# A macaron transformer block: first gate/up sums read unsplit copies of x, and loads of operands and of w_out move on the queue

## The chip, the cores and the metric

One core of one Trainium2 chip runs the whole program in one launch. The metric is device time in microseconds (us); lower is better. Before: median 2323.25 us of three runs (2322.42 to 2323.91).

## The reference, cut to what matters

x is 1024 tokens by 1024 columns, float32.

```python
x = LN1(alpha*x + 0.5*FFN1(x))              # FFN: (silu(x @ w_gate) * (x @ w_up)) @ w_down, 4096 wide
z = x @ w_in                                # q, k, v of 8 heads of 64, and the inputs of an RG-LRU
fox = causal softmax attention of q, k, v with forget gates (a bias cum[t] - cum[s] on the scores)
lru = gelu(gate) * RG_LRU(conv(u))
x = LN2(alpha*x + concat(fox, lru) @ w_out)
x = LN3(alpha*x + 0.5*FFN2(x))
```

## The kernel before, in words

Every float32 operand of a matmul is split in two: hi, a rounded copy that ACT (the scalar engine) casts, and lo = source - hi, which DVE (the vector engine) subtracts. A product is then three matmuls of 128x512 on PE (the tensor engine), written in lines 163, 164 and 165: hi by hi and the two cross terms. The two big products gate and up of each FFN go by a Strassen-like scheme with seven products of half-size blocks in place of eight. For a pair of 128-column blocks of w_gate and w_up, `weights` loads 128x8x256 raw weights on SP's queue (L364; a load of w_gate and one of w_up), forms t1, t2, t3, t4 from the quarters (L355) and splits each (ACT L349, DVE L350). There are 16 such pairs; in pairs 1 to 15 only weights are new.

Pair 0, `first_pair`, also builds the block sums of x. The rows of x are loaded (x2 tiles and `row` tiles), transposed on PE through PSUM (L249, tile `b`), and split into "11", "12", "22", "21" and the sums s1 = 22 + 21 (L449), s2 = s1 - 11 (L475), s3 = 11 - 21 (L479), s4 = 12 - s2 (L519). The tiles A, As and As4 hold the splits; `put` casts hi at once and queues the lo subtraction, and `do` issues the next one queued (L391). For s2, s3 and s4, blocks "11" and "12" are transposed a second time (`a11`, `a12`), since their first transposes have left PSUM by then and only their splits remain. After the sums come the additions of the products into the results (L436, L523, L524, L533, L544), and behind them the finish of the pair's result: DVE multiplies gate by up (L692), forms block sums of it for the next product (L695 to L699), and POOL stores them. `first_pair` runs in the order in which it is written; other parts are ordered by the scheduler.

While gate/up 1 runs, idle slots of the other engines prepare operands of FFN 2 and of w_out in DRAM. A step of `prepare` loads two `aux` tiles on SP (L272), subtracts (L290, DVE), splits (L278 on ACT, L279 on DVE) and stores to pre_d or wo_d on POOL's queue (GpSimd). `ready_pair` at the start of FFN 2 loads pre_d back (L556), and `ready_out_w` (L1119) loads the eight split tiles `w` of wo_d, 512 KB each.

The attention runs its 8 heads of 8 query tiles as 64 units in one loop over n. A unit's scores are L1158 (with kh) and L1159 (with kl); POOL masks the bias tile `cum` (L1162), DVE takes p = scores + cum and its maximum m (L1164), ACT the exponential (L1165), PE transposes p (L1179), and L1200 multiplies by v. Each head's load is eight DMAs on SP's queue: q, kh, kl of two halves, cum, v. In between the loop fills in output-projection tiles of the LRU half (`fill`), loads `w` at n = 45, 47, 49, 51 and the stored `mix` tiles at n in MIXES, and runs `out_tile`, the output projection. POOL stores mix to mix_d (L1216) after subtracting (L1213).

SP and POOL issue their DMAs in the order of the program; a DMA that waits on SP holds those behind it.

Of the kernel before, what the change touches and what calls it, by code (L numbers as in the profile page):

```python
# [59 lines left out]
class Block:  # L60
# [273 lines left out]
    def gate_up(self, wg, wu, h_d, rows, bank, tp, wsp, raws=None, later=None, aside=None, ready=None, steps=None):  # L334
# [26 lines left out]
        def weights(pair, view, w):  # L361

            r = self.raw([P, KT, 2 * P])
            nc.sync.dma_start(r, view[:, :, pair * 2 * P:(pair + 1) * 2 * P])  # L364
            b11, b12, b21, b22 = quarters(r)
            w["11"] = parts(b11)
            w["21"] = parts(b21)
            t1 = less(b12, b11)
            t2 = less(b22, t1)
            w["t2"] = parts(t2)  # L370
            w["t1"] = parts(t1)
            w["t3"] = parts(less(b22, b12))
            w["22"] = parts(b22)
            w["t4"] = parts(less(b21, t2))

        def first_pair(g, u):

            both = g, u
            q = {m: quarters(r) for m, r in zip(both, raws)}
            r1, r2 = rows[0:4], rows[4:NT]  # L380
            late = []

            def put(to, src):
                hi, lo = to
                nc.scalar.copy(hi, src)
                late.append((lo, src, hi))

            def do(n=1):
                for _ in range(n):
                    lo, src, hi = late.pop(0)  # L390
                    v.tensor_tensor(lo, src, f32(hi), ALU.subtract)  # L391

            def place(name, j):
                return tuple(x[:, :, j * P:(j + 1) * P] for x in A[name])

            def fill(m, n, src):
                m.w[n] = homes[n, m] if (n, m) in homes else two_blocks()
                put(m.w[n], src)

            homes = {(n, m): two_blocks() for n in ("11", "21", "t1") for m in both}  # L400
            t21 = [block() for _ in range(4)]
            t1, t2, t4, t3 = {}, {}, {}, {}
            for j in range(4):
                put(place("11", j), self.transposed(r1[j], 0, bank))
                do()
            put(place("12", 0), self.transposed(r1[0], 1, bank))
            fill(g, "11", q[g][0])
            do()
            for j in (1, 2):
                put(place("12", j), self.transposed(r1[j], 1, bank))  # L410
                do()
            fill(u, "11", q[u][0])
            do()
            put(place("12", 3), self.transposed(r1[3], 1, bank))
# [9 lines left out]
            s = [block() for _ in range(4)]  # L424
            fill(g, "t1", t1[g])
            do()
            nc.scalar.copy(g.s1, g.sum)
            fill(u, "t1", t1[u])
            do()
            t2[g] = less(q[g][3], t1[g])  # L430
            do()
            t2[u] = less(q[u][3], t1[u])
            a22, two = {}, {}

            def add_two(m):
                v.tensor_tensor(m.c[0], two[m], m.s1, ALU.add)  # L436

            def put_22(*js):
                for j in js:
                    put(place("22", j), a22[j])  # L440

            for j in range(4):
                nc.scalar.copy(t21[j], self.transposed(r2[j], 0, bank))
                a22[j] = self.transposed(r2[j], 1, bank)
                if j == 0:
                    nc.scalar.copy(u.s1, u.sum)
                else:
                    put(place("s1", j - 1), s[j - 1])
                v.tensor_tensor(s[j], a22[j], t21[j], ALU.add)  # L449
                if j:  # L450
                    do()
            put(place("s1", 3), s[3])
            two[g] = g.product("21", "12")
            put_22(0)
            do(2)
            two[u] = u.product("21", "12")
            add_two(g)
            later()
            put_22(1, 2, 3)
# [12 lines left out]
            four = {g: g.product("t4", "22")}  # L472

            def s2(j):
                v.tensor_tensor(s[j], s[j], a11[j], ALU.subtract)  # L475
                put(place("s2", j), s[j])

            def s3(j):
                v.tensor_tensor(t21[j], a11[j], t21[j], ALU.subtract)  # L479
# [33 lines left out]
            fill(g, "22", q[g][3])  # L513
            do()
            fill(u, "22", q[u][3])
            do(2)
# [10 lines left out]
            s4(0)  # L527
            nc.scalar.copy(u.u, u.sum)
            g.product("t3", "s3", g.sum)
            s4(1)  # L530
            do()
            for m in both:
                v.tensor_tensor(m.u, m.u, m.s5, ALU.add)  # L533
            s4(2)
            do()
            u.product("t3", "s3", u.sum)
            s4(3)
            do()
            add_seven(g)
            do()  # L540
            three = {m: m.product("22", "s4") for m in both}
            add_seven(u)
            for m in both:
                v.tensor_tensor(m.c[1], three[m], m.u, ALU.add)  # L544

        def ready_pair(g, u):

# [15 lines left out]
            for n in ("t4", "t2"):  # L563
                r = self.rawp.tile([P, 4, 4, P], F32R, tag="raw", name=self.nm("raw"))
                for i, m in enumerate(both):
                    fetch(n, m, (r[:, 2 * i], r[:, 2 * i + 1]))
# [111 lines left out]
        def halves(r):  # L678
            return r[:, 0:H], r[:, H:]

        pending = None
        for pair in range(FF // P // 2):
            if pair == 0:
                g0, h0, first, fifth, g1, h1, u = (self.row() for _ in range(7))
                homes = list(zip(halves(first), halves(first), halves(fifth)))
                gate, up = Matrix((g0, g1), *homes[0]), Matrix((h0, h1), *homes[1])
# [35 lines left out]
            for m in (gate, up):  # L722
# [399 lines left out]
    def attention(self, w_out, mixp, ln, normed):  # L1122
# [7 lines left out]
        with self.pool("att_p", 3) as pp, self.pool("att_t", 1) as tp, self.pool("att_pt", 6) as ptp, self.pool("att_qk", 2, side="right") as qkp:  # L1130
# [110 lines left out]
            for n in range(len(units) + AHEAD + 1):  # L1241
# [173 lines left out]
```

## Time and profile before

| | us |
|---|---|
| median of the runs | 2323.25 |
| the profiled execution | 2323.19 |
| its span, first to last instruction | 2321.5 |
| PE busy | 2298.7 (99% of the span) |
| DVE busy | 1635.6 (70%) |
| ACT busy | 1019.1 (44%) |
| POOL busy | 227.8 (10%) |
| mean granted PE clock | 0.997 |

The profiled execution is 1.7 us longer than its span and 0.06 us under the median. In the timeline rows the columns are the start in us, the duration, the engine, the line, the operation and its tiles, a count of like instructions, and in brackets how long the engine stood idle before and what released it. A matmul's row lasts 0.39 us, but the next one starts 0.227 us after it; likewise a DVE row of 0.68 us is followed 0.60 us later. The lines are those of the kernel before; from about line 1000 on the changed kernel's are 10 higher.

### The profile page before, as it was taken

Reading aid. Unit: us, or ns where it says so; the run is one execution under the profiler, and the core shown is the slowest. Engines: PE = TensorE matmul, PEld = TensorE weight load, DVE = VectorE, ACT = ScalarE, POOL = GpSimd, SP = SyncE. Lnnn points to the kernel's source line nnn. Section 1 sums busy time; section 2 is a strip of 40 time slices with the busy share of each in tenths; the row PEclk is TensorE's granted clock in tenths of the full one; section 3 lists DMA queues with packets and bytes.
Section 4 is the critical chain, followed back from the end, with each engine's and each line's share of the span. In section 5 each row is a group of like instructions: output and inputs, shape, how many; then the busy total and the mean of one; then the engine's idle time right before and its main releaser. Section 6 shows DMA issues by size and latency. Waiting matters only on the chain.

```text
span 2321.5 us, 28560 instructions
## 1 busy us (share of the span) xinstructions
PE 2298.7 (99%) x10705; PEld 1914.1 (82%) x10705; DVE 1635.6 (70%) x2521; ACT 1019.1 (44%) x1623; POOL 227.8 (10%) x388
## 2 busy tenths in 40 slices
PE   8999999999999999999999999999999999999998
PEld 7888888888888888888898788888888888888887
DVE  7867666666467788866667899565656665577886
ACT  5443434343344345453556755334333333344341
POOL 0121111100000000111133210000000000000000
PEclk9999999999999999999999999999999999999999
DMA  4444444433276433233274934232323232564542
GB/s 150 141 141 145 139 147 141 146 113 125 101 259 234 147 127 109 75 92 110 91 218 126 283 137 141 86 118 89 122 93 123 87 118 87 195 244 168 182 144 73
DMA packets 194444, 323.08 MB, mean 139 GB/s; under 512 B 10033, under 2 KB 115825, under 8 KB 194305
## 3 DMA queue, kind: packets, MB, share of 16 engines
q1 hardware_dynamic: 167712, 230.74, 30.9%
q0 software_dynamic: 26592, 90.51, 9.9%
q8 instruction: 84, 1.38, 0.3%
q14 instruction: 56, 0.45, 0.1%
HBM read 226.81 MB, written 94.40 MB: 138 GB/s over the span
## 4 chain that ended last, share of the span: by engine, by line
PE 81%; issue 10%; DVE 3%; DMA 3%; POOL 2%; ACT 1%; SPq 0%; POOLq 0%; DVEq 0%; ACTq 0%
PE x L163 7%; PE x L164 7%; PE x L165 7%; PE s L165 6%; PE s L164 6%; PE s L163 6%; PE a L165 6%; PE a L164 6%; PE a L163 6%; PE b L163 6%; PE b L164 6%; PE b L165 6%; PE a L1200 1%; PE a L1179 1%; PE a L1049 1%
## 5 line engine op out<-in xcount | busy, mean ns | idle before, releaser
L349 ACT CAST ws<-t 128x512 fp32r<-128x512 f32 x240 | 148.9, 623 | 374.2 <-PE b L164 253.0
L349 ACT CAST ws<-raw 128x512 fp32r<-128x512 f32 x180 | 111.0, 622 | 239.3 <-PE x L164 237.3
L350 DVE TENSOR_TENSOR ws<-t,ws 128x512 fp32r<-128x512 f32 x240 | 164.3, 686 | 56.4 <-ACT ws L349 50.6
L350 DVE TENSOR_TENSOR ws<-raw,ws 128x512 fp32r<-128x512 f32 x180 | 123.3, 688 | 114.4 <-ACT ws L349 110.3
L164 PE MATMUL a<-ws,ws 128*128 128x512 f32 x512 | 199.8, 390 | 0.2
L163 PE MATMUL a<-ws,ws 128*128 128x512 f32 x512 | 199.3, 390 | 0.4 <-ACT row L672 0.4
L163 PE MATMUL b<-As,ws 128*128 128x512 f32 x512 | 199.4, 389 | 0.2 <-ACT row L663 0.2
L164 PE MATMUL b<-As,ws 128*128 128x512 f32 x512 | 199.3, 389 | 0.0
L165 PE MATMUL b<-As,ws 128*128 128x512 f32 x512 | 199.2, 389 | 0.0
L165 PE MATMUL a<-ws,ws 128*128 128x512 f32 x512 | 199.2, 389 | 0.0
L163 PE MATMUL x<-As,ws 128*128 128x512 f32 x504 | 196.6, 390 | 2.1 <-ACT row L659 2.0
L164 PE MATMUL x<-As,ws 128*128 128x512 f32 x504 | 196.1, 389 | 0.0
L165 PE MATMUL x<-As,ws 128*128 128x512 f32 x504 | 196.1, 389 | 0.0
L163 PE MATMUL x<-A,ws 128*128 128x512 f32 x496 | 193.3, 390 | 0.0
L165 PE MATMUL x<-A,ws 128*128 128x512 f32 x496 | 193.0, 389 | 0.0
L164 PE MATMUL x<-A,ws 128*128 128x512 f32 x496 | 193.0, 389 | 0.0
L772 ACT CAST ws<-raw 128x1024 fp32r<-128x1024 f32 x112 | 117.4, 1050 | 157.8 <-PE a L164 87.2
L775 DVE TENSOR_TENSOR ws<-raw,ws 128x1024 fp32r<-128x1024 f32 x112 | 136.6, 1220 | 53.0 <-ACT ws L772 52.6
L702 POOL DMA_DIRECT2D h_d<-row x96 | 68.9, 719 | 968.5 <-DVE row L696 928.4
L163 PE MATMUL s<-ws,ws 128*128 128x512 f32 x384 | 149.5, 389 | 0.0
L165 PE MATMUL s<-ws,ws 128*128 128x512 f32 x384 | 149.4, 389 | 0.0
L164 PE MATMUL s<-ws,ws 128*128 128x512 f32 x384 | 149.4, 389 | 0.0
(295 smaller groups left out, 5252.7 us busy)
## 6 DMA issues: line engine op xcount, KB each, us to landing
raw<-h_d SPq DMA_DIRECT2D x56, 1024.0 KB, 5.4
h_d<-row POOLq DMA_DIRECT2D x96, 512.0 KB, 3.5
wd<-in_ffn_w_down_dram SPq DMA_DIRECT2D x32, 1024.0 KB, 7.5
raw<-in_ffn_w_gate_dram SPq DMA_DIRECT2D x30, 1024.0 KB, 5.3
raw<-in_ffn_w_up_dram SPq DMA_DIRECT2D x30, 1024.0 KB, 5.3
h_d<-row POOLq DMA_DIRECT2D x32, 256.0 KB, 2.7
raw<-in_w_in_dram SPq DMA_DIRECT2D x16, 512.0 KB, 4.9
pre_d<-ws POOLq DMA_DIRECT2D x28, 256.0 KB, 2.7
```

Source lines behind the costliest of these rows:

```text
L163: mm(out, ah, bh, start=first, stop=False, skip_group_check=goes_on)
L164: mm(out, ah, bl, start=False, stop=False, skip_group_check=goes_on)
L165: mm(out, al, bh, start=False, stop=last, skip_group_check=goes_on)
L349: nc.scalar.copy(hi, src)
L350: v.tensor_tensor(lo, src, f32(hi), ALU.subtract)
L702: nc.gpsimd.dma_start(d[:, 2 * n:2 * n + 2], t.rearrange("p (r t) -> p r t", r=2))
L772: cast = nc.scalar.copy(hi, src)
L775: self.mark = v.tensor_tensor(lo, src, f32(hi), ALU.subtract)
L1049: nc.tensor.matmul(pa[:, 0:width], xh, wh[:, 0:width], start=k == 0, stop=False)
L1179: nc.tensor.transpose(pa[:, (j % 4) * P:(j % 4 + 1) * P], p[:, j * P:(j + 1) * P], self.ident)
L1200: mm(pv[:, ps], vt[:, j, :], pts[h, qt][j // 4][l][:, j % 4, ps], start=j == 0 and l == 0, stop=j == last and l == 1)
```

## The change

In `first_pair`, ACT keeps a plain copy of each first transpose of "11" and "12" in the row of x that it came from, and s2, s3 and s4 read these copies instead of second transposes. The product "22"·s4 adds onto the product "t1"·"s1" in PSUM (m.z), so that the two additions of L533 go; `add_two` and `add_seven` come behind s4. Steps of `prepare` are tied behind the latest raw weight load, `ready_pair`'s first loads behind a later one of the program, and the w_out tiles are loaded at n = 36 to 39.

```diff
             for j in range(4):
-                put(place("11", j), self.transposed(r1[j], 0, bank))
+                pt = self.transposed(r1[j], 0, bank)
+                put(place("11", j), pt)
+                nc.scalar.copy(unsplit(r1[j], 0), pt)
                 do()
...
+            def put_12(j):
+                keep.append((unsplit(r1[j], 1), self.transposed(r1[j], 1, bank)))
+                put(place("12", j), keep[-1][1])
+
+            def keep_12():
+                nc.scalar.copy(*keep.pop(0))
...
-            add_two(g)
...
-            a11 = [self.transposed(r1[j], 0, bank) for j in range(2)]
             u.z = u.product("t1", "s1")
-            add_two(u)
-            a11 += [self.transposed(r1[j], 0, bank) for j in (2, 3)]
...
-                v.tensor_tensor(s[j], s[j], a11[j], ALU.subtract)
+                v.tensor_tensor(s[j], s[j], unsplit(r1[j], 0), ALU.subtract)
...
-            a12 = [self.transposed(r1[j], 1, bank) for j in range(4)]
...
-                v.tensor_tensor(s[j], a12[j], s[j], ALU.subtract)
+                v.tensor_tensor(s[j], unsplit(r1[j], 1), s[j], ALU.subtract)
...
-            for m in both:
-                v.tensor_tensor(m.u, m.u, m.s5, ALU.add)
...
+            for m in both:
+                add_two(m)
             add_seven(g)
-            do()
-            three = {m: m.product("22", "s4") for m in both}
+            for m in both:
+                m.product("22", "s4", m.z)
             add_seven(u)
             for m in both:
-                v.tensor_tensor(m.c[1], three[m], m.u, ALU.add)
+                v.tensor_tensor(m.c[1], m.z, m.u, ALU.add)
...
-            for n in ("11", "21", "t1"):
-                for m in both:
-                    fetch(n, m, two_blocks())
+            with self.tc.issue_after(self.fetched.ins):
+                for n in ("11", "21", "t1"):
+                    for m in both:
+                        fetch(n, m, two_blocks())
...
                     if steps and step in ("two", "five"):
-                        next(steps, None)
+                        with self.tc.issue_after(self.weight_load.ins):
+                            next(steps, None)
...
-                if 45 <= n < 53 and n % 2:
+                if 36 <= n < 40:
                     w_fox.append(next(w_steps))
```

`fill(g, "22", ...)` and `fill(u, "22", ...)` also move two places down among the s4 steps.

On DVE, at the start of pair 0, where the last weights of "t1" are split (L391) and the sums s1 begin; before:

```order
L391 TENSOR_TENSOR ws_178<-raw_136,ws_177 128x512
L290 TENSOR_TENSOR aux_775<-aux_775,aux_773 128x256
L391 TENSOR_TENSOR ws_180<-t_261,ws_179 128x512
L355 TENSOR_TENSOR t_289<-raw_135,t_261 128x512
L391 TENSOR_TENSOR ws_182<-t_264,ws_181 128x512
L355 TENSOR_TENSOR t_292<-raw_136,t_264 128x512
L449 TENSOR_TENSOR ws_280<-b_300,ws_183 128x512
```

and now:

```order
L391 TENSOR_TENSOR ws_178<-raw_136,ws_177 128x512
L391 TENSOR_TENSOR ws_180<-t_265,ws_179 128x512
L355 TENSOR_TENSOR t_296<-raw_135,t_265 128x512
L391 TENSOR_TENSOR ws_182<-t_268,ws_181 128x512
L355 TENSOR_TENSOR t_299<-raw_136,t_268 128x512
L464 TENSOR_TENSOR ws_284<-b_307,ws_183 128x512
```

The step of `prepare` (L290) has left this place; it now stands in pair 1.

On DVE, where pair 0's result is finished and pair 1's operand t2 is split (the L350 row that reads the newest t); before, with L350 of t2 ahead of the last five additions L695 to L699:

```order
L692 TENSOR_TENSOR row_167<-row_167,row_166 128x1024
L350 TENSOR_TENSOR ws_684<-t_681,ws_683 128x512
L695 TENSOR_TENSOR row_168<-row_163,row_167 128x512
L696 TENSOR_TENSOR row_168<-row_163,row_167 128x512
L697 TENSOR_TENSOR row_162<-row_163,row_167 128x512
L698 TENSOR_TENSOR row_163<-row_163 128x512
L699 TENSOR_TENSOR row_167<-row_167 128x512
```

and now, where the same five are L704 to L708:

```order
L704 TENSOR_TENSOR row_168<-row_163,row_167 128x512
L705 TENSOR_TENSOR row_168<-row_163,row_167 128x512
L706 TENSOR_TENSOR row_162<-row_163,row_167 128x512
L707 TENSOR_TENSOR row_163<-row_163 128x512
L708 TENSOR_TENSOR row_167<-row_167 128x512
L355 TENSOR_TENSOR t_643<-raw_633 128x512
L666 TENSOR_TENSOR row_627<-b_723,row_628 128x512
L355 TENSOR_TENSOR t_645<-raw_633,t_643 128x512
L355 TENSOR_TENSOR t_655<-raw_633 128x512
L355 TENSOR_TENSOR t_665<-raw_633,t_645 128x512
L350 TENSOR_TENSOR ws_648<-t_645,ws_647 128x512
```

The five additions have moved ahead of t2 and its split.

On SP, behind the load of head 5 (heads are counted from 0), where the tiles of mix, w and head 6 (q, kh, kl, cum) are loaded; before:

```order
L1269 DMA mix_11083<-mix_d 128x1024
L1269 DMA mix_11084<-mix_d 128x1024
L1119 DMA w_11254<-wo_d 128x1024
L1119 DMA w_11255<-wo_d 128x1024
L1140 DMA kh_11106<-k_d 64x1024
L1139 DMA q_11105<-q_d 64x1024
L1141 DMA kl_11107<-k_d 64x1024
```

and now:

```order
L1129 DMA w_10944<-wo_d 128x1024
L1129 DMA w_10945<-wo_d 128x1024
L1129 DMA w_10969<-wo_d 128x1024
L1129 DMA w_10970<-wo_d 128x1024
L1129 DMA w_11007<-wo_d 128x1024
L1129 DMA w_11008<-wo_d 128x1024
L1129 DMA w_11027<-wo_d 128x1024
L1129 DMA w_11028<-wo_d 128x1024
L1279 DMA mix_11063<-mix_d 128x1024
L1279 DMA mix_11064<-mix_d 128x1024
L1149 DMA q_11085<-q_d 64x1024
L1150 DMA kh_11086<-k_d 64x1024
```

Six more loads of `w` stand ahead of head 6; the later places of `w`, behind heads 6 and 7, are empty.

More of the change, by code (lines that the diff above doesn't have):

```diff
@@ L363, in weights @@
             r = self.raw([P, KT, 2 * P])
-            nc.sync.dma_start(r, view[:, :, pair * 2 * P:(pair + 1) * 2 * P])
+            self.weight_load = nc.sync.dma_start(r, view[:, :, pair * 2 * P:(pair + 1) * 2 * P])
             b11, b12, b21, b22 = quarters(r)
@@ L403, in first_pair @@
             for j in range(4):
-                put(place("11", j), self.transposed(r1[j], 0, bank))
-                do()
-            put(place("12", 0), self.transposed(r1[0], 1, bank))
+                pt = self.transposed(r1[j], 0, bank)
+                put(place("11", j), pt)
+                nc.scalar.copy(unsplit(r1[j], 0), pt)
+                do()
+            keep = []
+            def put_12(j):
[3 more added lines that the diff above has]
+                nc.scalar.copy(*keep.pop(0))
+            put_12(0)
             fill(g, "11", q[g][0])
@@ L409, in first_pair @@
             for j in (1, 2):
-                put(place("12", j), self.transposed(r1[j], 1, bank))
+                put_12(j)
                 do()
@@ L413, in first_pair @@
             do()
-            put(place("12", 3), self.transposed(r1[3], 1, bank))
+            put_12(3)
             do(2)
@@ L424, in first_pair @@
             s = [block() for _ in range(4)]
+            keep_12()
             fill(g, "t1", t1[g])
@@ L428, in first_pair @@
             fill(u, "t1", t1[u])
+            keep_12()
+            keep_12()
             do()
@@ L446, in first_pair @@
                     nc.scalar.copy(u.s1, u.sum)
+                    keep_12()
                 else:
@@ L474, in s2 @@
             def s2(j):
-                v.tensor_tensor(s[j], s[j], a11[j], ALU.subtract)
+                v.tensor_tensor(s[j], s[j], unsplit(r1[j], 0), ALU.subtract)
                 put(place("s2", j), s[j])
             def s3(j):
-                v.tensor_tensor(t21[j], a11[j], t21[j], ALU.subtract)
+                v.tensor_tensor(t21[j], unsplit(r1[j], 0), t21[j], ALU.subtract)
                 put(place("s3", j), t21[j])
@@ L512, in first_pair @@
             do()
-            fill(g, "22", q[g][3])
             do()
-            fill(u, "22", q[u][3])
-            do(2)
             def s4(j):
-                v.tensor_tensor(s[j], a12[j], s[j], ALU.subtract)
+                v.tensor_tensor(s[j], unsplit(r1[j], 1), s[j], ALU.subtract)
                 put(place("s4", j), s[j])
@@ L527, in first_pair @@
             s4(0)
+            fill(g, "22", q[g][3])
             nc.scalar.copy(u.u, u.sum)
@@ L530, in first_pair @@
             s4(1)
-            do()
-            for m in both:
-                v.tensor_tensor(m.u, m.u, m.s5, ALU.add)
+            fill(u, "22", q[u][3])
+            do(2)
             s4(2)
@@ L537, in first_pair @@
             s4(3)
-            do()
+            do(3)
+            for m in both:
+                add_two(m)
             add_seven(g)
-            do()
-            three = {m: m.product("22", "s4") for m in both}
+            for m in both:
+                m.product("22", "s4", m.z)
             add_seven(u)
             for m in both:
-                v.tensor_tensor(m.c[1], three[m], m.u, ALU.add)
+                v.tensor_tensor(m.c[1], m.z, m.u, ALU.add)
         def ready_pair(g, u):
@@ L558, in fetch @@
                 m.w[n] = to
-            for n in ("11", "21", "t1"):
-                for m in both:
-                    fetch(n, m, two_blocks())
[L563 to L566, printed above, removed]
+            with self.tc.issue_after(self.fetched.ins):
+                for n in ("11", "21", "t1"):
+                    for m in both:
+                        fetch(n, m, two_blocks())
+                for n in ("t4", "t2"):
+                    r = self.rawp.tile([P, 4, 4, P], F32R, tag="raw", name=self.nm("raw"))
+                    for i, m in enumerate(both):
+                        fetch(n, m, (r[:, 2 * i], r[:, 2 * i + 1]))
             t21 = [block() for _ in range(4)]
@@ L684, in gate_up @@
                 g0, h0, first, fifth, g1, h1, u = (self.row() for _ in range(7))
-                homes = list(zip(halves(first), halves(first), halves(fifth)))
-                gate, up = Matrix((g0, g1), *homes[0]), Matrix((h0, h1), *homes[1])
+                gate, up = (Matrix((r, e), r[:, 0:H], x, y) for r, e, x, y in zip((g0, h0), (g1, h1), halves(first), halves(fifth)))
             else:
```

## The prediction

> **What bounds the kernel now.** I read the page first, then the waits of PE, then a table of windows, and last the timelines of the places that the diff touches.
>
> ```profile
> span 2321.5 us, 28560 instructions
> PE 2298.7 (99%) x10705; PEld 1914.1 (82%) x10705; DVE 1635.6 (70%) x2521; ACT 1019.1 (44%) x1623; POOL 227.8 (10%) x388
> ...
> PE b L163 <- ACT ws L443: 2.8, 1, 2.8
> PE s L1158 <- DVE m L1164: 2.4, 7, 0.9
> ...
> PE a L1179 <- DVE pt L1184: 1.0, 3, 0.6
> PE a L1179 <- ACT p L1165: 0.5, 1, 0.5
> ```
>
> PE is busy 2298.7 of 2321.5 us, so 22.8 us is all that better feeding could give. Its longest wait, 2.8 us, stands once, in gate/up 1's pair 0; the next ones are in the attention. These are the two places that the change touches on PE's path. The windows (us, PE, PEld, DVE, ACT, POOL busy, granted PE clock, DMA share, GB/s):
>
> ```profile
> 22.19:25.60 3.41, 1.41 (x6) 1.20 (x7) 3.32 (x7) 2.56 (x5) 0.00 (x0) 1.00 0.00 0
> 25.60:29.01 3.41, 3.41 (x10) 2.68 (x9) 2.97 (x5) 2.63 (x6) 0.00 (x0) 0.50 0.00 0
> 29.01:50.00 20.99, 20.99 (x104) 17.55 (x104) 19.59 (x33) 11.91 (x21) 0.00 (x0) 1.00 0.01 2
> 50.00:75.00 25.00, 24.73 (x114) 19.86 (x113) 24.78 (x40) 12.53 (x20) 2.94 (x4) 1.00 0.47 163
> 75.00:1290.00 1215.00, 1210.62 (x5712) 1012.37 (x5711) 844.86 (x1345) 544.17 (x875) 159.73 (x264) 1.00 0.43 140
> 1290.00:1345.00 55.00, 51.46 (x346) 43.82 (x345) 44.78 (x110) 40.39 (x99) 13.88 (x36) 1.00 0.91 285
> ```
>
> Two things to see. From 29 to 75 us DVE is nearly as full as PE (19.59 of 20.99, then 24.78 of 25.00), while over the next 1215 us it is at 70%: at the start two engines bound together. And after the window in which PE worked 1.41 of 3.41 us its clock was granted at 0.50 for one window of 3.41 us.
>
> **Gate/up 1, PE's side.** The chain ahead of the 2.80 us wait and the second transposes, in PE's, DVE's and ACT's timelines:
>
> ```profile
> 15.62 1.29 DVE L391 TENSOR_TENSOR ws<-raw,ws 128x512 fp32r<-128x512 f32 x2
> 19.57 0.43 DVE L290 TENSOR_TENSOR aux<-aux,aux 128x256 f32<-128x256 f32 x1 [2.66 <-DMA aux<-in_ffn_w_gate_dram]
> 19.91 0.68 DVE L391 TENSOR_TENSOR ws<-t,ws 128x512 fp32r<-128x512 f32 x1
> ...
> 23.56 0.58 ACT L443 COPY ws<-b 128x512 f32<-128x512 f32 x1
> ...
> 24.19 0.50 PE L163 MATMUL b<-A,ws 128*128 128x512 f32 x1 [2.80 <-ACT ws L443]
> ...
> 34.09 1.03 PE L249 MATMUL b<-ident,row 128*128 128x128 f32 x8
> ...
> 37.70 1.03 PE L249 MATMUL b<-ident,row 128*128 128x128 f32 x8
> ...
> 49.47 1.91 PE L249 MATMUL b<-ident,row 128*128 128x128 f32 x16
> ```
>
> DVE stood 2.66 us for the aux tiles of an operand step, whose loads SP had issued ahead; the sums s1, ACT's copies and PE's next product stood behind that. With the step tied behind the raw loads, L290 leaves this place: the 2.80 us go, and with them the idle window and the half clock, 3.41 x 0.5 = 1.7 us. The 32 second transposes go: 8, 8 and 16 of 0.109 us (34.09 to the next matmul is 0.87), 3.5 us. PE alone could be 2.8 + 1.7 + 3.5 = 8.0 us earlier. ACT's eight copies of 0.58 us (the L443 row has the shape) are 4.6 us; ACT is idle 9 us from 29.01 to 50.00 alone, so I cost them at nothing; without that cover they would hold the casts behind them, 4.6 us at most.
>
> **Gate/up 1, DVE's side.** DVE cannot follow by 8.0. The place where that shows is pair 1's operand t2, whose lo part the first L164 of its product reads:
>
> ```profile
> 28.51 0.69 DVE L436 TENSOR_TENSOR row<-b,row 128x512 f32<-128x512 f32 x1 [0.35 <-PE b L165]
> 31.56 0.69 DVE L436 TENSOR_TENSOR row<-b,row 128x512 f32<-128x512 f32 x1 [0.56 <-PE b L165]
> 38.34 0.69 DVE L475 TENSOR_TENSOR ws<-ws,b 128x512 f32<-128x512 f32 x1 [0.42 <-PE b L249]
> ...
> 52.17 1.29 DVE L533 TENSOR_TENSOR row<-row,row 128x512 f32<-128x512 f32 x2
> ...
> 64.47 1.22 DVE L692 TENSOR_TENSOR row<-row,row 128x1024 f32<-128x1024 f32 x1
> 65.61 0.68 DVE L350 TENSOR_TENSOR ws<-t,ws 128x512 fp32r<-128x512 f32 x1
> 66.21 0.68 DVE L695 TENSOR_TENSOR row<-row,row 128x512 f32<-128x512 f32 x1
> ...
> 68.27 0.39 PE L164 MATMUL x<-As,ws 128*128 128x512 f32 x1
> ```
>
> From the L391 at 19.91 up to t2's split at 65.61 the order of before has 67 rows of 0.60 us (65.61 to 66.21) and two of 1.14 (64.47 to 65.61): 42.5 of 45.7 us, 3.2 idle. The order of the changed kernel has 72 and two ahead of the same split: the two L533 (52.17) are gone, and the five finishing additions, an L666 and an L355 have moved ahead. That is 45.5 us. They can begin when the L391 of 15.62 ends, at 16.9 instead of 19.91. Of the idle time, 1.33 us (the three waits quoted) belongs to steps that are moved or read no transposes now; 1.9 stays. So the split stands at 16.9 + 45.5 + 1.9 = 64.3, done at 65.0, and PE's L164 comes at about 65.0 where it came at 68.27: a gain of 3.3 us, not 8.0. Bounds: with no idle at all 5.2, with all 3.2 of it again 2.0. I take 3.3, since the waits that remain are those of the same steps. From there DVE has 30% to spare again, and PE keeps what it has gained: nothing in pairs 1 to 15 gives it back, if the operand steps behind the raw loads wait no longer on DVE than that spare; without that cover each such wait costs up to the 2.66 us of L290.
>
> PE now has 8.0 - 3.3 = 4.7 us of waiting spread ahead of that split: by the same rows some in pair 1's first products, most ahead of t2's. If two us of it fall into one window, the row after 22.19:25.60 says that a half-clock window follows, 1.7 us. The windows do not start with the kernel's steps, so I take three chances in ten, 0.5 us. The Trainium skill (TensorE: Matmul & The Clock Gate, Part 1: The HAM clock gate) has the clock fall only after about one whole idle window of 3.4 us; by that rule this term is 0 and the sum 0.5 us lower. This trace speaks against it: 1.41 us of work in the window did not keep the clock.
>
> **Attention.** Head 6's cum from issue to landing, the two loads of w behind head 6 on SP and their time to landing, and the rate at a full DMA in two windows:
>
> ```profile
> 1298.93 9.90 DMA cum<-cum_d
> ...
> 1301.94 2.12 SPq L1119 DMA_DIRECT2D w<-wo_d  x2
> ...
> DMA to landing us min/median/max: 9.5/10.3/11.0
> ...
> 1301.00:1311.00 10.00, 9.20 (x63) 7.56 (x62) 8.87 (x26) 9.04 (x24) 3.08 (x9) 1.00 1.04 286
> 1310.30:1311.40 1.10, 1.10 (x9) 0.97 (x8) 0.99 (x6) 1.10 (x5) 0.73 (x2) 1.00 1.03 417
> ```
>
> Six more w tiles, 6 x 0.524 MB = 3.15 MB, stand ahead of head 6's load on SP, and DMA is full from there on (share over 1), so they cannot be hidden. At 417 GB/s, a stretch of such large rows, they take 7.5 us; at 286, a mixed stretch, 11.0. Head 6's cum landed at 1298.93 + 9.90 = 1308.8, and will land at 1316.3 to 1319.8. What it meets:
>
> ```profile
> 1313.11 1.23 DVE L1164 CUSTOM_DVE_ANT_0 p<-s,cum 128x1024 f32<-128x1024 f32 x1
> ...
> 1322.40 0.40 PE L1159 MATMUL s<-kl,q 128*128 128x512 f32 x1
> ...
> 1323.52 1.11 POOL L1216 DMA_DIRECT2D mix_d<-mix  x2
> 1324.64 0.30 POOL L1162 TENSOR_SCALAR_AFFINE_SELECT cum<-cum 128x128 f32<-128x128 f32 x1
> 1325.82 1.21 DVE L1164 CUSTOM_DVE_ANT_0 p<-s,cum 128x1024 f32<-128x1024 f32 x1
> ...
> 1338.20 0.50 PE L165 MATMUL a<-w,mix 128*128 128x512 f32 x1 [0.18 <-DMA mix<-mix_d]
> ```
>
> Head 6's first p ran at 1313.11 and will run at about 1316.3 + 0.3 for the mask: 3.5 us late. The order puts 2.2 us more of head 5's products ahead of head 6's scores, so PE has something to do meanwhile. Between this p and head 7's first, 12.7 us later, the order has only some 8 us of PE's work, so a delay of 3.5 can be made up there, and head 7 decides. Only four more w stand ahead of it (the order of before has two between the heads), 2.1 MB, 5.0 us at 417 GB/s; and of those two the second, landing 9.5 and 11.0 us after issues at 1301.9 and 1302.8, took 2.4 us where 0.524 MB take 1.3 at that rate. Without that loss the four cost 3.9. Head 7's first scores were through at 1322.40 + 0.40 = 1322.8, and yet p came at 1325.82, since POOL's mask at 1324.64 stood behind two stores of mix. In the new order those stores belong to values that come earlier, and POOL is free. So p comes at 1322.8 + 3.9 + 0.3 = 1327.0, 1.2 us late, or 2.3 with the loss. Behind it the way to the output projection is as long as before, and the wait for mix at 1338.20 (0.18 idle, some 0.3 against the cadence) goes, since no w stands ahead of that load. I take 0.9 of loss, at the rate that such large rows had. The bounds are -1 (PE's waits of 1.0 and 0.5 us for pt and p shrink by more than the loads cost) and +5 (286 GB/s).
>
> `ready_pair`'s eight loads, 2.1 MB, come behind all this, at 1335 to 1345:
>
> ```profile
> 1403.81 0.50 PE L163 MATMUL b<-A,ws 128*128 128x512 f32 x1
> ```
>
> Their first reader is FFN 2's first product at 1403.81; at 285 GB/s they need 7 us. Nothing.
>
> **The sum,** against the profiled execution's 2323.2 us (span 2321.5 and 1.7 around it; the median of the runs is the same to 0.1): -3.3 + 0.5 + 0.9 = -1.9, so 2321.3 us. About 0.2%, 4.65 us, is what a measurement of this kernel can tell from no change; the lines are at 2318.6 and 2327.9.
>
> **The rivals.** (1) DVE is no bound: it fills its idle time and the steps in front of t2 are not needed in that order, so that PE takes all 8.0. For it: 1.33 of DVE's waits are for PE itself. Against it: the count of 74 rows. Then 2323.2 - 8.0 + 0.9 = 2316.1. (2) The w loads starve the attention. If DMA moves them at 286 GB/s, head 6's p is 7.0 us late (1319.8 + 0.3); PE has no other work, and head 7's four w at the same rate (7.3 us) leave about 2 us of a second stall: 9.0 lost against 3.3 - 0.5 gained, 2323.2 + 6.2 = 2329.4. It decides once head 6's cum lands later than about 1318 on the old clock, where the loss passes the gain. For it: the share of 1.04 in both windows, and that everything goes by one queue. The Trainium skill (DMA: Bandwidth & Descriptors, Queues, rings and completion order) says that each DMA engine takes a ring's descriptors in ring order; by that, head 6's load cannot overtake the w. The trace agrees: cum needed 9.90 us from its issue behind two w. Against it: 417 GB/s where large rows flow, and the POOL hold that goes. (3) The change doesn't do what it says at the start: ACT's copies of "12" stand ahead of the copies of t21 that PE waited for, so the 2.80 us remain in part and DVE's earlier start is eaten. Then 0 to 1 gained and 0.9 lost: 2322.6 to 2324.1, no change.
>
> **How the numbers follow.** Forecast 0.5, rival 1 0.2, rival 2 0.12, rival 3 0.18. The forecast's own range runs from 2323.2 - 5.2 - 1.0 = 2317.0 to 2323.2 - 2.0 + 1.7 + 2.1 = 2325.0 (the later head 7, less the mix wait, in the last term); about a quarter of it (0.12) lies under 2318.6. Faster: 0.2 + 0.12 = 0.32; slower: rival 2, 0.12; the rest, 0.56, is no change that can be told. The range for 8 in 10 reaches to rival 1 at 2316.1 and to 2325.0, and leaves rival 2 out.
>
> **What would show it.** In the new profile: no wait of PE near 24 us and no 0.50 window behind it; 64 transposes with `row` in gate/up 1 instead of 96; DVE without idle from 20 to 65 us; PE waiting for L350 ahead of pair 1's t2, and that product's L164 near 65.0. In the attention, head 6's cum landing near 1316 less the 3 us gained, PE idle ahead of head 6's first transposes, and no p of head 7 waiting for POOL. I am wrong if pair 1's t2 product starts before 63.5 (DVE was no bound), if PE still waits 2 us ahead of "21" times "12", or if the attention costs more than the start gains.

## The result, and the profile after

The changed kernel is slower: median 2329.55 us of eight runs (2327.21 to 2332.75) against 2322.91 (2320.59 to 2325.56) for eight of the kernel before, ratio 1.0029 [1.002, 1.0038], 6.6 us. The profiled execution took 2327.49 us, 4.3 more than that of before, its span 4.3 more as well; it is among the fastest of the eight, so the rows below show less than the whole loss. The page's first lines and then the waits of PE (us in total, times, longest), of after:

```profile
span 2325.8 us, 28505 instructions
PE 2298.8 (99%) x10673; PEld 1911.7 (82%) x10673; DVE 1634.3 (70%) x2519; ACT 1023.3 (44%) x1631; POOL 228.0 (10%) x388
```

```profile
PE a L163 <- ACT mix L1222: 2.6, 1, 2.6
PE s L1168 <- DVE m L1174: 2.4, 6, 1.0
PE x L163 <- ACT ws L349: 2.2, 1, 2.2
PE s L1168 <- DMA kh<-k_d: 1.8, 1, 1.8
```

The 2.8 us wait of before (L443) is gone. In its place stand three: one at the start (L349), and two in and behind the attention that before did not have (kh, mix). The windows over the same stretches of after, columns as before:

```profile
22.19:25.60 3.41, 3.41 (x17) 2.81 (x16) 3.32 (x7) 2.83 (x7) 0.00 (x0) 1.00 0.00 0
25.60:29.01 3.41, 3.41 (x17) 2.83 (x16) 3.25 (x6) 1.53 (x4) 0.00 (x0) 1.00 0.00 0
29.01:50.00 20.99, 20.57 (x92) 16.72 (x91) 20.82 (x35) 13.81 (x25) 0.00 (x0) 1.00 0.14 41
50.00:75.00 25.00, 21.94 (x86) 16.75 (x85) 22.99 (x38) 12.07 (x19) 2.94 (x4) 0.93 0.50 176
75.00:1290.00 1215.00, 1212.07 (x5734) 1014.20 (x5733) 844.69 (x1348) 545.33 (x879) 160.52 (x266) 1.00 0.42 139
1290.00:1345.00 55.00, 45.70 (x288) 37.74 (x287) 39.38 (x96) 35.59 (x88) 13.00 (x33) 0.97 0.93 298
```

At the start PE works through where it stood idle, and DVE is full from 29 to 50 us (20.82 of 20.99; before 19.59). In the last row PE is busy 45.70 of 55 us, where it was 51.46: the loss is there. One mark divides the two. It is a score matmul early in the attention, which came at 1234.56 in before and 4.1 us earlier in after:

```profile
1234.56 0.50 PE L1158 MATMUL s<-kh,q 128*128 128x512 f32 x1 [0.31 <-DVE m L1164]
```

```profile
1230.47 0.50 PE L1168 MATMUL s<-kh,q 128*128 128x512 f32 x1 [0.31 <-DVE m L1174]
```

So everything ahead of it gained 4.1, and what follows lost 4.3 + 4.1 = 8.4. In PE's timeline of after the loss stands in two pieces, around head 6's scores and in the output projection:

```profile
1311.32 1.19 PE L1168 MATMUL s<-kh,q 128*128 128x512 f32 x2 [1.81 <-DMA kh<-k_d]
...
1337.48 0.48 PE L163 MATMUL a<-w,mix 128*128 128x512 f32 x1
...
1342.37 0.50 PE L163 MATMUL a<-w,mix 128*128 128x512 f32 x1 [2.55 <-ACT mix L1222]
```

The first product of the output tile (1337.48) stood at 1335.93 in before:

```profile
1335.93 0.48 PE L163 MATMUL a<-w,mix 128*128 128x512 f32 x1
```

That is 1.55 later by the clock, 5.6 later against a start that was 4.1 earlier. Then PE waits 2.55 for mix, where before it waited 0.18 (L165). Together 8.0 of the 8.4. Some of the first piece is the clock's: it was halved for one window behind the wait for kh, and 3.01 us of work at half speed lose at most 1.5.

```profile
1310.92:1314.33 3.41, 3.01 (x11) 2.78 (x12) 0.00 (x0) 0.37 (x2) 0.00 (x0) 0.50 1.09 271
```

The second piece is POOL's doing. The views are of after: POOL, DVE and ACT ahead of that wait.

```profile
1338.73 1.04 POOL L192 TENSOR_SCALAR gb<-gb 128x1024 f32<-128x1024 f32 x1 [3.64 <-DMA gb<-in_ln_g_dram]
1339.74 0.28 POOL L1172 TENSOR_SCALAR_AFFINE_SELECT cum<-cum 128x128 f32<-128x128 f32 x1
```

```profile
1340.06 0.82 DVE L1174 CUSTOM_DVE_ANT_0 p<-s,cum 128x640 f32<-128x640 f32 x1 [2.79 <-POOL cum L1172]
```

```profile
1340.99 0.83 ACT L1175 ACTIVATE p<-p,m 128x640 f32<-128x640 f32 x1 [2.80 <-DVE m L1174]
```

L192 scales the gains of the layer norm (`gb`), which SP loads behind the mix tiles. POOL runs in order, stood 3.64 us for that load, and the mask of a unit of head 7 stood behind it; DVE's p, ACT's exponential and the last mix tile followed. In before the mask of the same unit, and the next one, came first:

```profile
1335.20 0.29 POOL L1162 TENSOR_SCALAR_AFFINE_SELECT cum<-cum 128x128 f32<-128x128 f32 x1 [1.65 <-DVE m L1164]
1336.54 0.29 POOL L1162 TENSOR_SCALAR_AFFINE_SELECT cum<-cum 128x128 f32<-128x128 f32 x1 [1.05 <-DVE m L1164]
...
1340.59 1.05 POOL L192 TENSOR_SCALAR gb<-gb 128x1024 f32<-128x1024 f32 x1 [2.23 <-DMA gb<-in_ln_g_dram]
```

With the w loads moved, the scheduler has put L192 ahead of two masks that used to stand before it.

### The profile page after: what moved, and what is told of

Same layout as the page of the kernel before. It is cut to its first block, busy times and chain, and to the rows that moved or that the text cites. A ratio compares the mean times of both kernels' runs of the same rounds, so it can differ in the third digit from the quotient of the medians.

```text
span 2325.8 us, 28505 instructions
## 1 busy us (share of the span) xinstructions
PE 2298.8 (99%) x10673; PEld 1911.7 (82%) x10673; DVE 1634.3 (70%) x2519; ACT 1023.3 (44%) x1631; POOL 228.0 (10%) x388
## 4 chain that ended last, share of the span: by engine, by line
PE 85%; issue 6%; DVE 3%; DMA 3%; POOL 1%; ACT 1%; SPq 0%; DVEq 0%; POOLq 0%; ACTq 0%
PE x L165 8%; PE x L163 8%; PE x L164 8%; PE b L163 7%; PE b L165 7%; PE b L164 7%; PE s L164 6%; PE s L165 6%; PE s L163 6%; PE a L163 6%; PE a L165 6%; PE a L164 6%; PE a L1210 1%; PE a L1189 1%; DMA wd<-in_ffn_w_down_dram 1%
## 5 line engine op out<-in xcount | busy, mean ns | idle before, releaser
L349 ACT CAST ws<-t 128x512 fp32r<-128x512 f32 x240 | 148.5, 623 | 372.8 <-PE b L164 257.8
L349 ACT CAST ws<-raw 128x512 fp32r<-128x512 f32 x180 | 110.8, 622 | 240.7 <-PE x L164 236.3
L350 DVE TENSOR_TENSOR ws<-t,ws 128x512 fp32r<-128x512 f32 x240 | 164.6, 687 | 56.9 <-ACT ws L349 52.0
L350 DVE TENSOR_TENSOR ws<-raw,ws 128x512 fp32r<-128x512 f32 x180 | 123.4, 688 | 114.7 <-ACT ws L349 110.7
L164 PE MATMUL a<-ws,ws 128*128 128x512 f32 x512 | 199.6, 390 | 0.2
L164 PE MATMUL b<-As,ws 128*128 128x512 f32 x512 | 199.3, 389 | 0.4 <-DVE As L391 0.4
L165 PE MATMUL a<-ws,ws 128*128 128x512 f32 x512 | 199.2, 389 | 0.0
L165 PE MATMUL b<-As,ws 128*128 128x512 f32 x512 | 199.2, 389 | 0.0
L165 PE MATMUL x<-As,ws 128*128 128x512 f32 x504 | 197.0, 391 | 0.1
L164 PE MATMUL x<-As,ws 128*128 128x512 f32 x504 | 196.6, 390 | 0.0
L165 PE MATMUL x<-A,ws 128*128 128x512 f32 x496 | 193.2, 390 | 0.7 <-DVE ws L350 0.5
L164 PE MATMUL x<-A,ws 128*128 128x512 f32 x496 | 193.0, 389 | 0.0
L164 PE MATMUL s<-ws,ws 128*128 128x512 f32 x384 | 149.5, 389 | 0.2 <-DVE ws L785 0.2
L165 PE MATMUL s<-ws,ws 128*128 128x512 f32 x384 | 149.4, 389 | 0.0
```

The costliest lines, as they stand in the source:

```text
L164: mm(out, ah, bl, start=False, stop=False, skip_group_check=goes_on)
L165: mm(out, al, bh, start=False, stop=last, skip_group_check=goes_on)
```

## The experiments

Times are medians over several rounds, beside the kernel before on the same chip; the profiled execution is one of them. The theory after the result: the start gains about what was forecast, and the moved w loads cost 9 to 10 us by two ways, head 6's load behind six more w, and POOL's hold. The rival: the rework of `first_pair` also costs, and the attention only shows it.

**The two halves of the change apart.** *first_only*: the kernel before with the new `first_pair` alone (unsplit copies, no second transposes, additions behind s4), steps and w as before.

```diff
-            a11 = [self.transposed(r1[j], 0, bank) for j in range(2)]
...
-                v.tensor_tensor(s[j], s[j], a11[j], ALU.subtract)
+                v.tensor_tensor(s[j], s[j], unsplit(r1[j], 0), ALU.subtract)
...
+            for m in both:
+                add_two(m)
```

> Only the first pair's part on the kernel before: plain copies, no second transposes, additions behind s4. Operand steps, w and ready_pair's loads as before. Queue theory (DVE's early wait for aux is what the start's gain comes from, the late w loads cost nothing here): PE's 2.8 us wait near 24 us stays, gain 1 to 2 us (2 additions of 0.60 and what PE's transposes held), attention as before: ratio 0.9991 to 0.9997. Rival (transposes are the gain): 3.5 us, ratio 0.9985.

Measured 2323.66 against 2322.74, ratio 1.0005 [0.9996, 1.0013]. PE still waits at the old place (2.85 at 25.27), and now at t2 too; the waits of PE in this kernel:

```profile
PE b L163 <- ACT ws L457: 2.9, 1, 2.9
PE x L163 <- ACT ws L349: 2.2, 1, 2.2
```

The 32 transposes less gain nothing alone: PE stands at the old wait as before, and once more at t2.

*w_only*: the kernel before with the w loads moved alone.

```diff
-                if 45 <= n < 53 and n % 2:
+                if 36 <= n < 40:
```

> Only the loads of w moved to n = 36 to 39 on the kernel before. Queue theory: the attention loses all of what the changed kernel lost there, 8 us: head 6's first score waits some 2 us for kh, a half-clock window follows, and 2.5 us of PE's wait near the first output tile come from POOL's scaling of gb: ratio 1.0030 to 1.0040. Rival (the moved loads are hidden, the loss comes from ready_pair's loads or the earlier start): within 1 us, ratio 0.9996 to 1.0004.

Measured 2331.57 against 2322.74, ratio 1.0033 [1.0021, 1.0046]: 8.8 us lost without any other edit. Both waits are there, in a profiled execution (2332.96) that is the slowest of the five:

```profile
PE a L163 <- ACT mix L1212: 4.3, 1, 4.3
...
PE s L1158 <- DMA kh<-k_d: 1.9, 1, 1.9
```

*w_back*: the changed kernel with the w loads where they were.

```diff
-                if 36 <= n < 40:
+                if 45 <= n < 53 and n % 2:
```

> The changed kernel with the loads of w back at n = 45, 47, 49, 51. Queue theory: the start's 4.1 us remain and the attention is as before: ratio 0.9980 to 0.9985. Rival (other moves cost in the attention): ratio 1.001 or more.

Measured 2319.83 against 2322.74, ratio 0.9987 [0.9979, 0.9996]: 2.9 us gained. Neither the kh nor the mix wait is left. After's 6.6 less this -2.9 is 9.5 for the moved loads, and *w_only*'s 8.8 agrees. The rival falls: nothing else in the change costs anything that these runs can tell.

**What the moved loads cost by each way.** *gb_tied*: the changed kernel, but POOL's scaling of `gb` is tied behind the mask of a late unit; the w loads stay moved.

```diff
+                    if n == 57:
+                        with self.tc.issue_after(self.mask.ins):
+                            nc.gpsimd.tensor_scalar(self.gb[0], self.gb[0], -1.0, 1.0, op0=ALU.mult, op1=ALU.mult)
```

> The changed kernel with POOL's scaling of gb tied behind the mask of unit 57, w still at n = 36 to 39. Theory that this scaling, waiting for its DMA ahead of a mask, is a cost of its own: PE's wait of 2.55 us ahead of the first output tile goes, 2 to 2.6 us less than the changed kernel (ratio 1.0018 against 1.0029). Rival (the mask or the rows behind it are late anyway): no more than 0.5 us less.

Measured 2326.05 against 2322.74, ratio 1.0011 [1.0002, 1.002]. PE's timeline:

```profile
1310.76 0.70 PE L1168 MATMUL s<-kh,q 128*128 128x512 f32 x2 [2.26 <-DMA kh<-k_d]
...
1339.91 0.50 PE L165 MATMUL a<-w,mix 128*128 128x512 f32 x1 [0.48 <-DVE mix L1223]
```

The wait ahead of the output tile is 0.48 where it was 2.55, head 6's is still there. From +6.6 to +3.3 us: some 3 of the 9.5 are POOL's hold.

*w43_gb*: *gb_tied*, and the w loads at a later place, two tiles ahead of head 6 and six ahead of head 7.

```diff
-                if 36 <= n < 40:
+                if 43 <= n < 47:
```

> The changed kernel with POOL's scaling of gb tied behind the mask of unit 57, and the loads of w at n = 43 to 46: two of the eight stand ahead of head 6's load, six ahead of head 7's. Theory that head 6, which came first behind the six more loads, was what starved: head 6's cum lands some 7 us sooner, PE's 2 us wait for kh goes, head 7 is no later than with w at 36 to 39: ratio 0.999 to 0.9998, 3 to 5 us less than with the scaling tied alone (1.0011). Rival (any order with w ahead of a head loses as much, head 7 now waits instead): ratio 1.0005 or more.

Measured 2321.17 against 2322.07, ratio 0.9995 [0.9986, 1.0004]. Of the load's wait 0.64 us is left:

```profile
1320.04 0.47 PE L1169 MATMUL s<-kl,q 128*128 128x512 f32 x1 [0.64 <-DMA kl<-k_d]
```

So head 6 behind eight w is some 4 us of the 9.5. The intervals of *gb_tied* and *w43_gb* overlap at their edges, and that of *w_back* lies across the latter: whether some third part of 2 us remains can't be told.

**Where the start's gain comes from.** *steps_only*: the kernel before, with nothing but the steps of `prepare` tied behind the raw loads.

```diff
-            nc.sync.dma_start(r, view[:, :, pair * 2 * P:(pair + 1) * 2 * P])
+            self.weight_load = nc.sync.dma_start(r, view[:, :, pair * 2 * P:(pair + 1) * 2 * P])
...
-                        next(steps, None)
+                        with self.tc.issue_after(self.weight_load.ins):
+                            next(steps, None)
```

> Only the operand steps tied behind the raw weight loads, on the kernel before; the first pair's sums, w and ready_pair's loads as before. Queue theory (DVE's wait for aux is most of the start's gain): PE's wait near 24 us falls from 2.8 to under 0.5 us and the half-clock window behind it goes, 3 to 4 us less: ratio 0.9982 to 0.9988. Rival (the two parts are needed together, since the second transposes and the additions then hold DVE and PE): 1 us or less, ratio 0.9995 or more.

Measured 2318.39 against 2322.07, ratio 0.9982 [0.9973, 0.9991]: 3.7 us, as much as *w_back* within the intervals. Where before had 2.80 idle there is

```profile
22.29 0.50 PE L163 MATMUL b<-A,ws 128*128 128x512 f32 x1 [0.15 <-ACT ws L443]
```

Within what these runs can tell, the whole gain of the start is the tie, an edit at two places.

**Can PE have the rest?** In *w_back* PE stands 2.2 us ahead of t2 for DVE, as in after. *pool_finish*: *w_back* with pair 0's five finishing additions on POOL, which is idle there.

```diff
+                e = nc.gpsimd if pair == 0 and ready is None else v
-                v.tensor_tensor(u[:, 0:H], a11, a22, ALU.add)
+                e.tensor_tensor(u[:, 0:H], a11, a22, ALU.add)
...
```

> The changed kernel with the loads of w back at n = 45, 47, 49, 51, and the five finishing additions of gate/up 1's pair 0 on POOL in place of DVE. Theory that DVE bounds the start through what stands ahead of t2's split: t2 comes six rows of 0.60 us sooner, PE's wait of 2.2 us ahead of its product goes: 2 to 2.5 us less than with w back alone, ratio 0.9976 to 0.9980 against 0.9987. Rival (PE's wait is not DVE's row order, but the raw load or ACT): no change against w back.

Measured 2322.77 against 2322.07, ratio 1.0004 [0.9995, 1.0012]: *w_back*'s gain is gone. DVE and POOL in this kernel, at the same time:

```profile
59.74 1.79 DVE L355 TENSOR_TENSOR t<-raw 128x512 f32<-128x512 f32 x1
61.45 1.51 DVE L290 TENSOR_TENSOR aux<-aux,aux 128x256 f32<-128x256 f32 x1
62.88 1.75 DVE L355 TENSOR_TENSOR t<-raw,t 128x512 f32<-128x512 f32 x1
```

```profile
59.37 1.61 POOL L705 TENSOR_TENSOR row<-row,row 128x512 f32<-128x512 f32 x1 [57.99 <-DVE row L701]
60.94 1.73 POOL L706 TENSOR_TENSOR row<-row,row 128x512 f32<-128x512 f32 x1
```

An L355 of that shape takes 0.69 us in after (63.90); beside POOL's additions it took 1.75. Over these three rows DVE lost 1.1 + 1.1 + 1.06 = 3.3 us, and 2.1 more over the two L355 behind them (1.76 each); five additions of 0.60 had cost it 3.0. So the split of t2 came later, not sooner, and PE, behind its 2.2, waited a second time:

```profile
68.65 0.80 PE L165 MATMUL x<-As,ws 128*128 128x512 f32 x1 [2.52 <-DVE ws L350]
```

*late_finish* and *steps_late*: pair 0's finish is put off into pair 1 as that of the other pairs is, on *w_back* and on *steps_only*.

```diff
-                end()
+                if ready is not None:
+                    end()
+                else:
+                    pending = end
```

> The changed kernel with the loads of w back at n = 45, 47, 49, 51, and pair 0's finish (both L701 and the five additions) written behind pair 1's first product, so that DVE splits pair 1's t2 eight rows sooner. Theory that DVE's rows ahead of t2's split take the gain that PE's missing transposes offer: PE's wait of 2.2 us ahead of t2's product goes and no half-clock window can follow it: 2.2 to 3.5 us less than with w back alone (0.9987), ratio 0.9972 to 0.9978. Rival (the offer is lost elsewhere, or to contention): no change against w back.

> The kernel before with only the operand steps tied behind the raw loads and pair 0's finish written behind pair 1's first product. Theory as above: here the second transposes still stand on PE, PE hardly waits for DVE in pair 1, and the later finish gains nothing: within 0.7 us of the tied steps alone, ratio 0.9979 to 0.9985. Rival (the later finish frees something of its own): 1.5 us less or more, ratio under 0.9977.

Measured 2318.45 against 2321.86, 0.9984 [0.9975, 0.9992], and 2318.23 against 2321.86, 0.9984 [0.9975, 0.9993]. In *late_finish* the 2.2 ahead of t2 is gone, but PE now waits 3.9 for L669 in pair 1, and ACT, ahead of it, for a step of `prepare`:

```profile
PE x L163 <- ACT row L669: 3.9, 1, 3.9
```

```profile
84.44 0.41 ACT L278 CAST ws<-aux 128x256 fp32r<-128x256 f32 x1 [8.29 <-DMA aux<-in_ffn_w_gate_dram]
```

ACT stood 8.29 us for a tile that the tie had put behind a raw load on the queue (issued at 73.54, the tile's own load at 76.61). The prediction had named such a wait as the price of the tie, on DVE; here it came on ACT. This profiled execution, 2321.74, is the slowest of the eleven, 3.3 over their median, and has two half-clock windows from 88.72 on, so the wait need not be as long in the others.

*late_skip* and *wback_skip*: the steps begin only with pair 3, on *late_finish* and on *w_back*.

```diff
-                    if steps and step in ("two", "five"):
+                    if steps and pair >= 3 and step in ("two", "five"):
```

> The changed kernel with the loads of w back, pair 0's finish behind pair 1's first product, and the operand steps beginning with pair 3 in place of pair 1. Theory that the later finish freed PE at t2, and that its gain went again where ACT's cast L278 waits for an aux tile whose load lies behind a raw load and pair 0's stores: PE's wait of 3.9 us near 90 us and the half-clock windows behind it go, 2.5 to 4 us less than with the later finish alone (0.9984): ratio 0.9967 to 0.9974. Rival (DMA is full there, and the raw weights themselves come late): no change.

> The changed kernel with the loads of w back and the operand steps beginning with pair 3, the finish as in the changed kernel. Theory as above: PE's wait of 2.2 us ahead of t2 stays, since DVE's rows ahead of it stay: within 0.8 us of w back alone, ratio 0.9983 to 0.9990. Rival (the steps' aux loads, not DVE's rows, make that wait): 2 us less, ratio 0.9979 or less.

Measured 2314.61 against 2322.55, 0.9966 [0.9954, 0.9978], and 2319.86 against 2322.55, 0.9989 [0.9981, 0.9998]. From 15 to 100 us PE waits once in *late_skip*:

```profile
50.51 0.50 PE L164 MATMUL b<-As,ws 128*128 128x512 f32 x1 [0.45 <-DVE As L391]
```

It beats both kernels, the one before by 7.9 us. It is the changed kernel with the w loads put back, pair 0's finish put off, and the steps from pair 3. *wback_skip* gains no more than *w_back*: the later steps help only once the finish is off DVE's path.

*old_skip*: the same two edits on *steps_only*, that is with the second transposes and the old order of the additions, and without the tie of `ready_pair`'s loads.

> The kernel before with the steps tied, pair 0's finish put off and the steps begun with pair 3: the fastest version so far without the rework of the first pair, so that only the second transposes and the order of the additions differ. Theory: PE has no wait left in the first 100 us with either finish, so beginning the steps later gives nothing more, and what the fastest version has over this one is PE's own work, 32 transposes of 0.109 us, 3.5 us: 3.7 us faster than before (2 to 5), ratio 0.9984. Rival: the gain of the fastest version comes from beginning the steps later, and the rework gives nothing: 7 to 8 us faster than before, ratio 0.9967.

Measured 2317.48 against 2322.16, 0.9981 [0.9972, 0.999]: 4.7 us gained, not 7 to 8. PE waits nowhere from 15 to 110 us, and its 32 second transposes still stand there, the last 16 of them in this row:

```profile
45.81 1.91 PE L249 MATMUL b<-ident,row 128*128 128x128 f32 x16
```

The 3.2 us between 7.9 and 4.7 are near the 3.5 of the transposes. The two intervals overlap by a little, so the size is not firm, but the rival, by which the later start of the steps gives all of it, doesn't hold.

## Why the prediction was wrong

**The start was right.** Its working put t2's split at 64.3 and 3.3 us of gain for the product that reads it. In DVE's and PE's timelines of after:

```profile
64.50 0.69 DVE L350 TENSOR_TENSOR ws<-t,ws 128x512 fp32r<-128x512 f32 x1
```

```profile
64.14 0.50 PE L163 MATMUL x<-As,ws 128*128 128x512 f32 x1 [2.20 <-ACT ws L349]
65.25 0.79 PE L165 MATMUL x<-As,ws 128*128 128x512 f32 x1
```

The split came at 64.50, and its 72 and two rows began at 17.20, where the working had 16.9. Its reader is the L165 (the prediction took the L164 in front of it): before it stood at 68.50, so 3.25 earlier. Rival 1 falls with this. Rival 3 falls too: the wait near 24 us is gone. The sum of -3.3 and 0.5 is -2.8; *w_back*, which has this part alone, measured -2.9. That they agree so closely is in part luck: of the 4.1 that after had gained by the score mark, 2.4 stood at the end of pair 1 (DVE's last L701 of it at 102.81, in before L692 at 105.20), and the other 1.7 came later; for that the working had no term, and its cause stays open. What gives the start's gain was left open there: the prediction took transposes, step and half clock as one gain of 8.0 for PE, cut down to 3.3 by DVE. *first_only* and *steps_only* show that the tied steps alone give as much.

**The half clock came, at the place that the 0.5 was for.** The half-clock stretches in a trace begin whole multiples of 3.413 us apart, so the throttle's own windows can be laid over it. Two of after, and two of *w_back*, whose wait is as long:

```profile
61.64:65.05 3.41, 1.21 (x5) 0.48 (x3) 3.41 (x6) 1.58 (x4) 1.68 (x3) 1.00 0.97 386
65.05:68.46 3.41, 3.32 (x9) 2.54 (x9) 3.41 (x8) 0.60 (x2) 0.00 (x0) 0.50 0.35 141
```

```profile
59.33:62.74 3.41, 2.42 (x11) 1.68 (x9) 3.41 (x7) 0.54 (x1) 2.60 (x4) 1.00 0.38 155
62.74:66.15 3.41, 2.16 (x8) 1.45 (x9) 3.41 (x7) 2.18 (x4) 0.34 (x1) 1.00 0.97 383
```

In after the wait of 2.20 lies in one window, which keeps 1.21 us of work, and the clock is halved in the next. In *w_back* the wait of 2.16 is split over two windows with 2.42 and 2.16 us of work, and the clock stays. So where the wait falls against these windows decided it, and that is what the prediction's three chances in ten stood for. Counted so in all fourteen profiled executions, from the first full-speed stretch that their traces record, every window with up to 1.41 us of PE's work had a half-clock window behind it, none with 1.92 or more had, and between these either came. A whole idle window, of which the Trainium skill speaks (TensorE: Matmul & The Clock Gate, Part 1: The HAM clock gate), was not needed: after 1.21 us of work in it the clock fell. In the profiled executions the start of *w_back* gained 6.1 (the score mark at 1228.42) and that of after 4.1; that of *w_back*, 2316.42, is the fastest of its eleven, 3.4 under their median.

**The attention is the step that failed,** 0.9 forecast, 9.5 measured, in three places. First, "I take 0.9 of loss, at the rate that such large rows had". SP issued head 6's cum at 1302.5 and head 7's at 1314.5, and these took 12.0 and 10.3 us to land:

```profile
L1153 SPq DMA_DIRECT2D cum<-cum_d x2: 325/325/325, 1302.5 to 1314.5; - x2
...
DMA to landing us min/median/max: 10.3/11.2/12.0
```

POOL's mask that reads head 6's began at 1314.54 after 3.82 idle, so the 12.0 is head 6's: 1302.5 + 12.0 = 1314.5. Before it was 1308.8: 5.7 less by the clock, and 9.8 against the earlier start. For 3.15 MB that is 320 GB/s, nearer to the lower of the two rates, 286, than to the 417 that was taken. On the old clock it landed at 1314.5 + 4.1 = 1318.6, past the 1318 from which rival 2 decides.

Second, "a delay of 3.5 can be made up there, and head 7 decides." DVE's rows for the first p of head 6 and of head 7 in after:

```profile
1315.33 1.22 DVE L1174 CUSTOM_DVE_ANT_0 p<-s,cum 128x1024 f32<-128x1024 f32 x1
```

```profile
1327.06 1.23 DVE L1174 CUSTOM_DVE_ANT_0 p<-s,cum 128x1024 f32<-128x1024 f32 x1 [0.32 <-PE s L1169]
```

Against 1313.11 and 1325.82, with the start's 4.1 added, head 6's is 6.3 late and head 7's 5.3: 1.0 was made up. Head 7's load did not decide; its p waited for PE's scores. Some 8 us of PE's work in 12.7 us was no spare of 4.7: PE was busy 9.23 of the 11.73 us between these two rows and stood the rest in single waits for DVE and ACT, the longest of them here, and head 7's scores came out of that chain:

```profile
1316.61 0.50 PE L1168 MATMUL s<-kh,q 128*128 128x512 f32 x1 [1.05 <-DVE m L1174]
...
1322.06 1.52 PE L1189 MATMUL a<-ident,p 128*128 128x128 f32 x9 [0.87 <-DVE pt L1194]
```

Third, POOL's hold, the other 2.4 us in the profile and some 3 by *gb_tied*. The prediction had "POOL is free" at head 7's first mask, because the stores of mix go. They did not go, in POOL's timeline of after:

```profile
1324.90 1.11 POOL L1226 DMA_DIRECT2D mix_d<-mix  x2
1326.02 0.30 POOL L1172 TENSOR_SCALAR_AFFINE_SELECT cum<-cum 128x128 f32<-128x128 f32 x1
```

There they cost nothing, as PE's scores came later still. The hold came at a later mask of head 7, where the prediction had not looked at what the scheduler would put ahead of it; it has no term for that. The two bounds of the attention, -1 and +5, were too narrow, and the range had only 2.1 of loss in it: even with +5 its upper end would have been 2327.9.

Rival 2's 2329.4 is nearly the time measured, but by chance: only its first part is what happened (head 6's p 7.0 late by the forecast, 6.3 measured, of which 5.6 reached the output tile). Its second stall, on head 7's w, did not come; POOL's hold, which no case of the prediction held, stood in its place.

## What to carry to other kernels

A load that is moved up on a queue is paid for by each load that then stands behind it: take the bytes at the slow mixed rate, and count a delay as made up only where the engine behind it has a backlog, not where it only has a low share of busy time. Where a scheduler orders the engines, look after each move at what it now puts ahead of short instructions in an engine's order, above all an instruction that waits for a DMA. An edit that shows nothing alone may be held by the next engine: the saved transposes gave nothing until the finish and the steps were off DVE's and ACT's path, and then some 3 us.

## What the runs showed of the hardware that was not expected

While POOL worked on float32 tiles in SBUF, DVE's work on such tiles slowed: its 128x512 additions went from 0.69 to 1.75 and 1.79 us and its 128x256 subtraction from 0.42 to 1.51, while POOL's 128x512 additions took 1.45 to 1.73 us each. Whether POOL lost too is not shown: no run has it do an addition of that size alone. Side by side they did 1/1.75 + 1/1.6 = 1.2 additions of that size per us, where DVE alone, at one in 0.60 us, does 1.7. Why they do so was not tried.
